# Attention scores kept negated, with a running minimum in place of a running maximum

## The chip, the cores and the metric

The kernel runs on one core of one Trainium2 chip. The metric is device time in microseconds. In the rows, PE is TensorE (PEld its weight loads), DVE is VectorE, ACT is ScalarE, POOL is GpSimd and SP is SyncE, which issues the DMAs; a "q" behind an engine's name is its sequencer.

## The reference, cut to what matters

One layer of a streaming encoder: an input projection, a short convolution beside four heads of differential attention, an output projection, a feed-forward block and a gated embedding. There are 2048 prompt rows and 32 sample rows. The part that the change touches is the softmax of the prompt's attention. Each head has two score maps (m = 0, 1):

```python
s = jnp.einsum('bqhmd,bkhmd->bhmqk', qf, kf)
dist = jnp.abs(q_pos[:, None] - k_pos[None, :]).astype(f)
bias = -alibi_slopes()[:, None, None] * dist
visible = (k_pos[None, :] // CHUNK) <= (q_pos[:, None] // CHUNK)
s = jnp.where(visible, s + bias[None, :, None], NEG_INF)
a = jax.nn.softmax(s, axis=-1)
attn = a[:, :, 0] - lam * a[:, :, 1]
o = jnp.einsum('bhqk,bkhd->bqhd', attn, v.astype(f))
```

## The kernel before, in words

**Stages.** The kernel first normalises and turns the prompt rows and projects them (to about 140 us), then does the attention of the four heads, woven with the projections of the next columns (about 140 to 895 us), and then the output projection, the feed-forward block and the gated embedding. Matrix products use pairs of 16-bit halves (high and low part), so that each product is three matmuls.

**A unit of attention.** `Unit(j, qb, idx)` is one head and one block of 128 query rows, so there are 4 x 16 units with two maps each, 128 maps in all. `scores` goes over a map's keys in chunks of at most 512 columns (320 chunks in all). Each chunk is two matmuls into a PSUM tile `sc` (three buffers; L617 and L618) and one DVE instruction, a custom `tensor_tensor_reduce` (L621). That one adds the position bias, multiplies by the head's scale `idd`, writes the scores `s` to SBUF and folds the largest of them into the [128, 1] tile `mx`, starting from the largest of the chunk before (`prev`) or from a constant in a map's first chunk. Reading the folded value out is a second DVE instruction in the trace. After the last chunk of a map POOL negates the maximum into `nm` (L628, recorded under the helper `ts`, L100), and ACT takes the exponential of the whole map with `nm` as its bias and sums it into `z` (L629).

**What follows a map.** Once both maps of a unit are there, `weigh` works out factors on POOL and DVE from the two `z` (tiles `ca`, `rz`, `sg`, `sgc`, `kk`; recorded at L102 and L583 to L586). In most units (`by_dma`) DVE combines the maps, ACT and DVE split them into halves (`s` at L170 and L105), a DMA on SP's queue turns them (`at`), and PE multiplies with the values (`smb`, L667 to L669) one unit later. The last seven units of head 3 turn the maps on PE (`turn_and_values`, tile `pta`). `subnorm` squares the result on ACT (`jko`, L518), takes a power on POOL (`rso`) and scales on DVE (`yg`).

**What runs beside it.** In the last seven units the fill is `early()`: the output projection's weights are split on ACT and DVE (`w`, L170 and L105, eight pairs of instructions of 128x1024) and the first two row tiles of that projection run.

**Order.** The program is traced by a planner (`schedule_with_timeline_sim=True`): it estimates times and sets the order of the instructions of every engine, by priority and by when they are ready in its estimate. A stretch at the start has its order written by hand on PE, ACT and DVE; the attention has not. Each engine works in order.

**Small tiles.** `t1` gives a [128, 1] tile of a pool with four buffers for each name (`sml1`, `bufs=4`), so the fifth `mx` takes the buffer of the first. Before the change `mx` is read by the next chunk's L621 or by POOL, and `nm` by ACT.

**Scales.** `q_scales` makes [128, 1] factors on POOL once for each head, among them `idd`.

Of the kernel before, what the change touches and what calls it, by code (L numbers as in the profile page):

```python
# [11 lines left out]
AF = mybir.ActivationFunctionType  # L12
ALU = mybir.AluOpType
# [16 lines left out]
BIG = 3.0e38  # L30
# [4 lines left out]
def hymba_step_kernel(  # L35
# [9 lines left out]
    V, A, G, T = nc.vector, nc.scalar, nc.gpsimd, nc.tensor  # L45
# [16 lines left out]
    cst = ctx.enter_context(tc.tile_pool(name="cst", bufs=1))  # L62
# [19 lines left out]
    def t1(tag, n=1, bufs=None):  # L82
        return here["small"].tile([P, n], F32, tag=tag, name=tag, bufs=bufs)
# [14 lines left out]
    def ts(eng, out, a, s1, op0, s2=None, op1=None):  # L98
        if op1 is None:
            eng.tensor_scalar(out=out, in0=a, scalar1=s1, scalar2=None, op0=op0)  # L100
        else:
            eng.tensor_scalar(out=out, in0=a, scalar1=s1, scalar2=s2, op0=op0, op1=op1)  # L102
# [4 lines left out]
    MUL, ADD, SUB, MAX = ALU.mult, ALU.add, ALU.subtract, ALU.max  # L107
# [55 lines left out]
    def prod(a, b, tag, c=1.0, pool=None):  # L163
        o = (pool or here["small"]).tile([P, 1], F32, tag=tag, name=tag)
        ts(G, o, a, b, MUL, c, MUL)
        return o
# [72 lines left out]
    gain = {}  # L239
# [86 lines left out]
    def k_group(c, tg, parts=1):  # L326
        j, h = c.j, heads[c.j]
        if tg == 0:
            h["ks"] = [pkv[j % 2].tile([P, S], F16, tag=f"ks{m}", name=f"ks{m}") for m in range(2)]
            h["ek"] = cst.tile([P, 1], F32, tag=f"ek{j % 2}", name="ek")  # L330
            h["swk"] = cst.tile([P, 1], F32, tag=f"swk{j % 2}", name="swk")
            G.tensor_copy(h["ek"], c.e)
            G.tensor_copy(h["swk"], c.sw)
            q_scales(order[place[GQ, j]])
# [62 lines left out]
    def q_scales(c):  # L397

        j, h = c.j, heads[c.j]
        h["iwq"] = cst.tile([P, 1], F32, tag=f"iwq{j % 2}", name="iwq")  # L400
        G.tensor_copy(h["iwq"], c.iw)
        a_ = prod(c.sw, h["swk"], "dd_a", 2.0 ** -37)
        a_ = prod(a_, gain["su"], "dd_b")
        h["dd"] = prod(a_, gain["su"], f"dd{j % 2}", 1.0, cst)
        a_ = prod(c.e, h["ek"], "id_a", 2.0 ** 9)
        a_ = prod(a_, gain["isu"], "id_b")
        h["idd"] = prod(a_, gain["isu"], f"idd{j % 2}", 1.0, cst)
        if j > 0:
            h["ratio"] = prod(h["dd"], heads[j - 1]["idd"], f"rat{j % 2}", 0.25, cst)

# [182 lines left out]
    class Unit:  # L593
# [13 lines left out]
        def scores(self):  # L607
            h, nk, qb = heads[self.j], self.nk, self.qb
            qs, q = h[("qs", qb // 4)], slice(qb % 4 * P, (qb % 4 + 1) * P)
            self.s, self.z = [], []  # L610
            for m in range(2):
                s_ = att.tile([P, S], F32, tag="s", bufs=4, name=f"s{m}")
                prev = None
                for c0, w_ in self.chunks:
                    ps = psc.tile([P, TG], F32, tag="sc", bufs=3, name="sc")
                    kc = h["ks"][m][:, c0:c0 + w_]
                    T.matmul(ps[:, :w_], qs[:, 2 * m, q], kc, start=True, stop=False)  # L617
                    T.matmul(ps[:, :w_], qs[:, 2 * m + 1, q], kc, start=False, stop=True)  # L618
                    mx = t1("mx")
                    b0 = S - nk + c0  # L620
                    ev = V.tensor_tensor_reduce(out=s_[:, c0:c0 + w_], in0=ps[:, :w_], in1=bias[:, b0:b0 + w_],  # L621
                                                scale=h["idd"], scalar=-BIG if prev is None else prev,
                                                op0=ADD, op1=MAX, accum_out=mx)
                    here["ev"] = getattr(ev, "ins", ev)
                    prev = mx
                    if c0 + w_ == nk:
                        nm, zz = t1("nm"), t1(f"z{m}")
                        ts(G, nm, prev, -1.0, MUL)  # L628
                        A.activation(out=s_[:, :nk], in_=s_[:, :nk], func=AF.Exp, bias=nm, accum_out=zz)  # L629
                        self.s.append(s_)  # L630
                        self.z.append(zz)
                    yield
# [234 lines left out]
    bias = att.tile([P, S], F32, tag="bias", bufs=1, name="bias")  # L867
# [983 lines left out]
```

## Time and profile before

| | us |
|---|---|
| median of 3 runs | 2536.61 (2534.45 to 2539.05) |
| the profiled execution, whole | 2533.34 |
| its span, first to last instruction | 2531.6 |
| PE busy in the span | 2456.3 |
| DVE busy | 1692.4 |
| ACT busy | 1139.1 |
| POOL busy | 756.0 |

The durations below come from the one profiled execution. Busy time counts overlapping instructions of an engine once. An idle time is put down to the engine and line that ended it. The granted clock is 1.00 at 2.4 GHz and 0.50 at 1.2 GHz.

### The profile page before, as it was taken

The numbers are of one execution on the slowest core, as the hardware profiler recorded it, in microseconds if no ns is written. First come the engines' busy times: TensorE is split into PE (matmuls) and PEld (weight loads), VectorE is DVE, ScalarE is ACT, GpSimd is POOL, SyncE is SP. The second block draws the span as 40 slices with busy tenths as digits, with TensorE's granted clock in tenths as the row PEclk, the third lists the DMA queues.
The fourth block names the chain that finished last, engine by engine and source line by source line (L and its number), as shares of the span: only waits on it lengthen the run. The fifth ranks groups of instructions, "written<-read, shape, count | busy, mean of one in ns | idle before, by whom it ended". The sixth has DMA issues, their size and how long they took to land.

```text
span 2531.6 us, 41709 instructions
## 1 busy us (share of the span) xinstructions
PE 2456.3 (97%) x15981; PEld 1283.6 (51%) x15981; DVE 1692.4 (67%) x2931; ACT 1139.1 (45%) x1977; POOL 756.0 (30%) x1307
## 2 busy tenths in 40 slices
PE   8999999999999799999999999999999999999998
PEld 7756655755745444444444444444444444444444
DVE  7578978969988857866665665654455547646664
ACT  5436635635643645643443443454233223425553
POOL 2143344334333434422222222210121102314442
PEclk9999999999999799999999999999999999999999
DMA  5134534524544335454444444366554547631221
GB/s 181 52 84 96 103 81 89 117 61 103 123 104 107 87 120 162 165 209 164 167 160 158 158 175 137 129 243 219 197 193 148 175 152 248 214 96 60 79 84 55
DMA packets 345083, 345.35 MB, mean 136 GB/s; under 512 B 150473, under 2 KB 241042, under 8 KB 344882
## 3 DMA queue, kind: packets, MB, share of 16 engines
q1 hardware_dynamic: 344882, 342.68, 44.4%
q8 instruction: 125, 2.05, 0.3%
q14 instruction: 76, 0.62, 0.1%
HBM read 206.68 MB, written 97.92 MB: 120 GB/s over the span
## 4 chain that ended last, share of the span: by engine, by line
PE 79%; DVE 9%; DMA 5%; ACT 3%; issue 3%; POOL 2%; SPq 0%; DVEq 0%; POOLq 0%; ACTq 0%
PE mm L1383 8%; PE mm L1385 8%; PE mm L1384 8%; PE mm L1614 7%; PE mm L1616 7%; PE mm L1615 7%; PE mm L959 4%; PE mm L961 4%; PE mm L963 4%; PE lin L317 4%; PE lin L318 4%; PE lin L319 4%; DVE s L105 2%; DVE s L621 2%; PE sc L617 1%
## 5 line engine op out<-in xcount | busy, mean ns | idle before, releaser
L1616 PE MATMUL mm<-v,hl 128*128 128x512 f16 x896 | 339.8, 380 | 3.1 <-DVE hl L1576 3.1
L1614 PE MATMUL mm<-v,hl 128*128 128x512 f16 x896 | 339.3, 380 | 2.1 <-ACT hl L1575 2.0
L1615 PE MATMUL mm<-v,hl 128*128 128x512 f16 x896 | 340.3, 380 | 0.0
L317 PE MATMUL lin<-uh,whl 128*128 128x512 f16 (+1 forms) x832 | 261.6, 330 | 4.1 <-DVE yt L105 1.3
L318 PE MATMUL lin<-ul,whl 128*128 128x512 f16 (+1 forms) x832 | 262.2, 330 | 0.7 <-DVE ul L105 0.7
L1576 DVE TENSOR_TENSOR hl<-fr,hl 128x1024 f16<-128x1024 f32 x112 | 150.0, 1349 | 168.1 <-ACT hl L1575 167.2
L319 PE MATMUL lin<-uh,whl 128*128 128x512 f16 (+1 forms) x832 | 261.7, 330 | 0.7 <-DVE whl L105 0.7
L1575 ACT ACTIVATE hl<-fr 128x1024 f16<-128x1024 f32 x112 | 116.7, 1051 | 301.7 <-PE mm L1616 278.2
L629 ACT ACTIVATE s<-s,nm 128x128 f32<-128x128 f32 (+15 forms) x128 | 153.5, 1199 | 167.1 <-POOL nm L100 166.4
L1383 PE MATMUL mm<-u,w 128*128 128x512 f16 x448 | 169.8, 379 | 1.1 <-ACT w L170 1.1
L1384 PE MATMUL mm<-u,w 128*128 128x512 f16 x448 | 169.8, 379 | 0.0
L1384 PE MATMUL mm<-u2b,w 128*128 128x512 f16 x448 | 169.8, 379 | 0.0
L1383 PE MATMUL mm<-u2b,w 128*128 128x512 f16 x448 | 169.2, 379 | 0.5 <-DMA u2b<-u_d 0.5
L1385 PE MATMUL mm<-u,w 128*128 128x512 f16 x448 | 168.8, 379 | 0.0
L1385 PE MATMUL mm<-u2b,w 128*128 128x512 f16 x448 | 168.5, 379 | 0.0
L621 DVE CUSTOM_DVE_ANT_0 s<-sc,bias,mx 128x512 f32<-128x512 f32 (+3 forms) x192 | 134.9, 702 | 16.0 <-PE sc L618 11.8
L1614 PEld LDWEIGHTS <-hl 128*128 128x128 f16 x896 | 87.8, 98 | 112.2 <-issue 6.9
L1616 PEld LDWEIGHTS <-hl 128*128 128x128 f16 x896 | 87.7, 98 | 110.7 <-DVE hl L1576 4.9
L1385 PEld LDWEIGHTS <-w 128*128 128x128 f16 x896 | 87.7, 98 | 105.3
L1615 PEld LDWEIGHTS <-hl 128*128 128x128 f16 x896 | 87.7, 98 | 104.5 <-issue 1.5
L1383 PEld LDWEIGHTS <-w 128*128 128x128 f16 x896 | 88.7, 99 | 100.2 <-ACT w L170 1.2
L1384 PEld LDWEIGHTS <-w 128*128 128x128 f16 x896 | 87.7, 98 | 99.2 <-issue 0.8
(464 smaller groups left out, 5847.8 us busy)
## 6 DMA issues: line engine op xcount, KB each, us to landing
ff_d<-e SPq DMA_DIRECT2D x224, 256.0 KB, 2.1
fr<-ff_d SPq DMA_DIRECT2D x112, 512.0 KB, 4.5
raw<-in_w_down_dram SPq DMA_DIRECT2D x80, 512.0 KB, 4.7
xt<-in_x_prompt_dram SPq DMA_DIRECT2D x32, 512.0 KB, 4.4
stg<-in_w_up_dram SPq DMA_DIRECT2D x16, 1024.0 KB, 6.5
stgd<-in_w_down_dram SPq DMA_DIRECT2D x16, 1024.0 KB, 5.6
stg<-in_w_in_dram SPq DMA_DIRECT2D x24, 512.0 KB, 5.3
h_d<-ht SPq DMA_DIRECT2D x16, 512.0 KB, 2.9
```

Source lines behind the costliest of these rows:

```text
L317: T.matmul(o, w[:, 0, ft], rh[:, ft, c], start=(ft == 0), stop=False)
L318: T.matmul(o, w[:, 0, ft], rl[:, ft, c], start=False, stop=False)
L319: T.matmul(o, w[:, 1, ft], rh[:, ft, c], start=False, stop=(ft == FT - 1))
L621: ev = V.tensor_tensor_reduce(out=s_[:, c0:c0 + w_], in0=ps[:, :w_], in1=bias[:, b0:b0 + w_], scale=h["idd"], scalar=-BIG if prev is None ...
L629: A.activation(out=s_[:, :nk], in_=s_[:, :nk], func=AF.Exp, bias=nm, accum_out=zz)
L1383: T.matmul(o, w[:, c, 0, kt], x[:, :, 0, kt], start=first and kt == 0, stop=False, skip_group_check=True)
L1384: T.matmul(o, w[:, c, 0, kt], x[:, :, 1, kt], start=False, stop=False, skip_group_check=True)
L1385: T.matmul(o, w[:, c, 1, kt], x[:, :, 0, kt], start=False, stop=kt == 3, skip_group_check=True)
L1576: V.tensor_tensor(out=hl[:, 1], in0=fr, in1=hl[:, 0], op=SUB)
L1614: T.matmul(ps, hl[:, 0, u % 2, c], v[:, 0], start=(u == 0), stop=False)
L1615: T.matmul(ps, hl[:, 0, u % 2, c], v[:, 1], start=False, stop=False)
L1616: T.matmul(ps, hl[:, 1, u % 2, c], v[:, 0], start=False, stop=(u == NU - 1))
```

## The change

The scale of the scores gets a minus sign (`nidd`), the fold becomes a minimum that starts from +3e38, and the exponential multiplies its input by -1 and adds the minimum itself: exp(-s' + min s') with s' = -s. POOL's negation and the tile `nm` go. One POOL instruction for each head is added, which makes `nidd`; `idd` stays, since the next head's `ratio` uses it.

```diff
         h["idd"] = prod(a_, gain["isu"], f"idd{j % 2}", 1.0, cst)
+        h["nidd"] = prod(a_, gain["isu"], f"nidd{j % 2}", -1.0, cst)
...
-                                                scale=h["idd"], scalar=-BIG if prev is None else prev,
-                                                op0=ADD, op1=MAX, accum_out=mx)
+                                                scale=h["nidd"], scalar=BIG if prev is None else prev,
+                                                op0=ADD, op1=ALU.min, accum_out=mx)
...
-                        nm, zz = t1("nm"), t1(f"z{m}")
-                        ts(G, nm, prev, -1.0, MUL)
-                        A.activation(out=s_[:, :nk], in_=s_[:, :nk], func=AF.Exp, bias=nm, accum_out=zz)
+
+                        zz = t1(f"z{m}")
+                        A.activation(out=s_[:, :nk], in_=s_[:, :nk], func=AF.Exp, bias=prev, scale=-1.0, accum_out=zz)
```

## Rows read from the trace of the kernel before

**Rows 1.** The page, part 1: busy us, share of the span, instructions.

```profile
PE 2456.3 (97%) x15981; PEld 1283.6 (51%) x15981; DVE 1692.4 (67%) x2931; ACT 1139.1 (45%) x1977; POOL 756.0 (30%) x1307
```

**Rows 2.** Windows: stretch, length, busy PE, PEld, DVE, ACT, POOL, clock, DMA share, GB/s.

```profile
140.00:810.00 670.00, 650.11 (x5429) 389.08 (x5427) 564.86 (x1367) 346.95 (x651) 269.12 (x605) 1.00 0.44 95
810.00:895.00 85.00, 64.19 (x433) 38.33 (x432) 63.90 (x159) 52.04 (x111) 36.97 (x96) 0.84 0.38 101
1200.00:2532.00 1332.00, 1317.12 (x6913) 604.80 (x6910) 764.94 (x988) 527.64 (x824) 313.77 (x383) 1.00 0.46 155
```

**Rows 3.** Waits of PE, 140 to 810 us: total us, times, longest.

```profile
PE smb L667 <- DMA at<-s: 6.5, 9, 1.1
PE sc L617 <- DVE mx L621: 4.2, 8, 1.0
```

**Rows 4.** Waits of PE, 810 to 895 us.

```profile
PE smb L667 <- DVE yg L100: 8.8, 3, 6.0
```

**Rows 5.** The chain that ended last: start us, us, what.

```profile
162.92 0.18 POOL nm L100
...
860.96 1.22 POOL nm L100
```

**Rows 6.** Groups by form, 140 to 895 us: busy us, mean ns, idle before.

```profile
L100 POOL TENSOR_SCALAR nm<-mx 128x1 f32<-128x1 f32 x128 | 39.1, 306 | 171.4 <-DVE mx L621 151.4 <-DVE e_w L100 10.7 <-DVE mcv L910 4.1
L621 DVE CUSTOM_DVE_ANT_0 s<-sc,bias,mx 128x512 f32<-128x512 f32 x120 | 96.3, 802 | 12.9 <-PE sc L618 10.5
L621 DVE CUSTOM_DVE_ANT_0 s<-sc,bias,idd 128x512 f32<-128x512 f32 x104 | 77.2, 743 | 5.1 <-PE sc L618 3.8 <-DMA at<-s 1.0
L364 ACT COPY kt<-ptk 128x512 f32<-128x512 f32 x12 | 6.9, 579 | 0.4 <-PE ptk L363 0.3
L170 ACT ACTIVATE at<-pta 128x512 f16<-128x512 f32 x4 | 2.4, 590 | 0.1
```

**Rows 7.** Timeline: start us, us, engine, line, out<-in, idle before.

```profile
821.92 0.08 DVE L621 DVE_READ_ACCUMULATOR2_ANT mx<- 128x1 f32 x1
822.09 0.22 POOL L100 TENSOR_SCALAR nm<-mx 128x1 f32<-128x1 f32 x1 [1.15 <-DVE mx L621]
822.35 1.25 ACT L629 ACTIVATE s<-s,nm 128x1152 f32<-128x1152 f32 x1 [3.85 <-POOL nm L100]
822.59 0.75 DVE L105 SCALAR_TENSOR_TENSOR s<-s,sgc,s 128x512 f32<-128x512 f32 x1
...
829.84 0.13 DVE L102 TENSOR_SCALAR i_wo<-e_wo 128x1 int32<-128x1 int32 x1
830.01 4.26 ACT L170 ACTIVATE w<-wst,i_wo 128x1024 f16<-128x1024 f32 x4 [0.42 <-DVE i_wo L102]
```

**Rows 8.** Timeline at 861 us, DVE and POOL.

```profile
860.82 1.28 DVE L105 SCALAR_TENSOR_TENSOR w<-wst,aswo,w 128x1024 f16<-128x1024 f32 x1
860.93 1.24 POOL L100 TENSOR_SCALAR nm<-mx 128x1 f32<-128x1 f32 x1
```

**Rows 9.** Waits of DVE, 140 to 810 us.

```profile
DVE rz L583 <- ACT s L629: 17.3, 18, 2.2
```

**Rows 10.** The tile idd on POOL: ns min/median/max, first and last start.

```profile
L102 POOL TENSOR_SCALAR idd<-id_b,g_i x4: 263/266/1322, 80.3 to 597.2; 128x1 f32<-128x1 f32 x4
```

**Rows 11.** Timeline: an exponential, and the fourth eviction after its maximum.

```profile
730.37 1.90 ACT L629 ACTIVATE s<-s,nm 128x1920 f32<-128x1920 f32 x1 [0.24 <-POOL nm L100]
...
733.13 0.52 DVE L621 CUSTOM_DVE_ANT_0 s<-sc,bias,mx 128x256 f32<-128x256 f32 x1
```

**Rows 12.** Timeline at 835 us, ACT and PE.

```profile
835.31 4.25 ACT L170 ACTIVATE w<-wst,aswo 128x1024 f16<-128x1024 f32 x4
839.47 0.26 ACT L518 ACTIVATE jko<-smb 128x128 f16<-128x128 f32 x1
...
841.53 0.27 PE L667 MATMUL smb<-vhl,at 128*128 128x128 f16 x1 [6.04 <-DVE yg L100]
```

**Rows 13.** Windows: the longest stretch of half clock there, columns of Rows 2.

```profile
836.22:846.46 10.24, 4.90 (x34) 3.71 (x34) 5.56 (x13) 7.85 (x16) 3.55 (x8) 0.50 0.30 58
```

## The prediction, as it was put on record

> **What bounds the kernel now.** I read the page's shares first: PE is busy for 97% of the span [rows 1], so an edit on DVE, POOL and ACT can win at most what PE lacks, and only where those engines make PE wait. The windows say where that is [rows 2]. From 1200 us on PE is busy for 1317.12 of 1332 us, and nothing of the change runs there. The attention falls into two parts. From 140 to 810 us PE is idle for 670 - 650.11 = 19.9 us at full clock, while DVE is busy for 564.86 of 670 us (84%). From 810 to 895 us, which I call the tail, PE is idle for 85 - 64.19 = 20.8 us, and the granted clock is 0.84 on the mean. So some 41 us of idle time, and what the half clock costs in the tail, are all that the change can reach.
>
> The waits of PE tell who holds it up. Before 810 us it waits 6.5 us in all for the turned maps `at`, which come out of the exponentials by way of combining, splitting and a DMA, and 4.2 us for a free `sc` buffer, which DVE's evictions give back [rows 3]. In the tail the largest is 8.8 us for `yg` [rows 4]. None of these names `nm`: POOL's negation is at least two steps away from PE. The chain of waits shows how often it matters all the same. I went through it from 140 to 900 us and found POOL's `nm` in 15 pieces, 5.64 us together; the first and the last stand in [rows 5]. The other 113 of the 128 are not on it.
>
> **The change part by part.**
>
> *The negation goes.* There are 128 of them, 39.1 us of POOL [rows 6]; POOL has idle time enough, so that alone is worth nothing. What counts is when the exponential starts. In the timeline the read-out of the maximum ends at 822.00, `nm` runs from 822.09 to 822.31 and the exponential starts at 822.35 [rows 7]: 0.35 us from DVE to ACT. Where ACT waits for DVE directly, DVE's `i_wo` ends at 829.97 and ACT starts at 830.01 [rows 7], which is 0.04 us. So a map whose exponential waits for `nm` gains 0.31 us. A further gain is the hold: `nm` at 860.93 takes 1.24 us instead of 0.22, and it ends 0.07 us after a DVE instruction that began 0.11 us before it and reads two tensors of SBUF [rows 8]. That is why the mean is 306 ns [rows 6] and the pieces on the chain are 5.64 us and not 15 x 0.22 = 3.3 us.
>
> The Trainium skill's page "SBUF — State Buffer" (section "Who interferes with whom") states the reason: a DVE instruction with two SBUF inputs contends with a GpSimd instruction that reads SBUF. By a price without it the chain's pieces would be 3.3 us, and with it they are the 5.64 us that the trace has; the trace agrees with the page.
>
> At the order as it is, the most that can go is the chain's pieces plus the longer way to POOL: 5.64 + 15 x (0.09 + 0.04 - 0.04) = 7.0 us. The least is nothing, where another path was as late. What is late next can be named. In the part before 810 us it is DVE: it stands 17.3 us, 18 times, at the head of `weigh` (`rz`) waiting for an exponential [rows 9], and 18 x 0.31 = 5.6 us of this goes; but the combining and splitting behind it is DVE's own work, 84% of the stretch. At 860.96 it is DVE's split of the weights, which runs anyway [rows 8]. With DVE so close behind, I take half of the upper end: -3.5 us.
>
> *The fold becomes a minimum.* 320 DVE instructions change their operation; the trace has no such form. Both sides are bounded by the two forms that it has, 743 ns with a constant as start and 802 ns with a tile, for 512 columns [rows 6]: 59 x 320 = 18.9 us of DVE time more or less. I take nothing, because another two-input instruction with a multiplication and an addition also takes 0.75 us for 512 columns [rows 7]: the columns set the time and not the operation. The read-out stays, 0.08 us [rows 7].
>
> *The exponential gets a scale of -1.* Its nearest rows are a copy without a factor, 579 ns, and a copy with a constant factor, 590 ns, on 512 columns [rows 6]: 11 x 128 = 1.4 us of ACT as the upper end, nothing as the lower. ACT is busy for 347 of 670 us [rows 2], which hides it; without that cover it would be the 1.4 us. I take 0.
>
> *`nidd` is added.* Four POOL instructions of 0.27 us like `idd` [rows 10], 1.1 us in all, or 5.3 us if each met the longest hold (1.32). They are made while the keys of a head are projected, ahead of the head's first unit; POOL is busy for 40% there. I take 0.
>
> *`mx` is held longer.* It is now freed by the exponential's end, and there are four buffers. So an L621 waits for the exponential of the map whose last chunk lies four chunks back. I set each of these 124 pairs side by side: the closest is an exponential that ends at 732.27 and an eviction at 733.13 [rows 11], so no pair would wait at today's times, by 0.86 us. If one waited, all of DVE's queue behind it (combining, splits, further evictions) and PE's `sc` would wait with it. I take 0, with up to 1 us for each pair that slips by 2 us.
>
> *The order may move.* The planner sets the order of PE, ACT and DVE by its own estimate, in which the exponentials are now ready earlier. No row shows the new order. A price for one misplaced block is in the tail: four splits of the weights, 4.25 us, stand on ACT before the square `jko`, and PE is idle for 6.04 us until `yg` [rows 12]; over the next 10.24 us the clock is at half while PE is busy for 4.90 us, work that takes half of that at full clock, so it costs 2.45 us [rows 13]. One such block is 4.25 + 2.45 = 6.7 us, in either direction. I take 0, since nothing in the rows says which way it goes.
>
> **Sum.** -3.5 + 0 + 0 + 0 + 0 + 0 = -3.5 us on the profiled execution, 2533.34 us (span 2531.6 and 1.74 us around it), so 2529.8 us there. The median of the runs shown is 3.3 us above that execution, so the prediction for a median is 2536.6 - 3.5 = 2533.1 us. About what a measurement of this kernel can tell from no change is 0.2%, or 5.1 us, so this is a gain inside it.
>
> **The rivals.**
>
> *The gain is all covered.* The 15 pieces go, and DVE is as late as before. For it: DVE is busy for 84% [rows 2], and the waits of PE name evictions and transfers [rows 3]. Against it: 18 waits of DVE end with an exponential [rows 9]. The time stays at 2536.6 us.
>
> *A better order in the tail (faster).* Exponentials that are ready sooner let the planner put `jko` ahead of the block of four splits. For it: the tail has 20.8 us of idle PE, by far the largest share of any stretch. Against it: the splits don't depend on `nm`. It is worth -6.7 us, and -10.2 where the chain's pieces, which were counted in the order as it is, can be had on top: 2526.4 to 2529.9, so some 2528 us.
>
> *A worse order in the tail (slower).* Exponentials that are ready sooner go before other ACT work, and the other four splits, too, land before a square that PE waits for. That is one block more, +6.7 us, and in another order the chain's pieces don't carry over: 2543.3 us. It decides from 5.1 us on, three quarters of a block with its clock. For it: the rows show that one such block costs PE 6 us. Against it: there are only eight splits, and four already stand badly.
>
> *The buffers of `mx` bind (slower).* If exponentials slip by 2 us against evictions, the closest pair waits 1.1 us; some eight such pairs give +9 - 3.5 = +5.5 us: 2542 us. Against it: exponentials come earlier by the change, not later.
>
> *The minimum runs at another speed (slower).* At 59 ns more, 18.9 us of DVE time, of which PE would see perhaps half, an estimate from DVE's 84%: +9.5 - 3.5 = +6 us, 2542.6 us.
>
> **How the numbers follow.** The forecast gets 0.37, the covered gain 0.11, the better order 0.30, the worse order 0.15, the buffers 0.04 and the slower minimum 0.03. Of the forecast's 0.37 the part beyond -5.1 us (its upper end is -7.0) is 0.03. So faster by over 0.2%: 0.30 + 0.03 = 0.33; within 0.2%: 0.34 + 0.11 = 0.45; slower: 0.15 + 0.04 + 0.03 = 0.22. The likeliest is the forecast, 2533.1 us; its own range is 2529.6 to 2536.6 us. The range takes in the better order below, to 2524 us (its far end and another 2.4 us, one more stretch of half clock saved), and the three slower rivals above, to 2545 us.
>
> **What would show it right or wrong.** No `nm` on POOL and 0.04 us from the read-out to the exponential; L621 still at 743 and 802 ns; `rz` waiting some 5 us less; PE's idle time before 810 us down by two or three us; no L621 that waits for an exponential. The order of ACT in the tail says whether one of the two order rivals came about: how long `yg` keeps PE waiting, and how long the clock is at half. The prediction is wrong if PE's idle time between 140 and 895 us moves by more than about 8 us either way, and then the order of an engine's instructions will have moved and not the price of one.

## The result, and the profile after

The changed kernel is slower: a median of 2551.81 us (2550.49 to 2558.08, 4 runs) against 2535.55 us (2534.45 to 2539.05, 4 runs) for the kernel before on the same chip, a ratio of 1.0066 with a 95% interval of 1.0054 to 1.0078. The forecast was 2533.1 us, and the time lies 7 us above the upper end of its range.

In the rows of after, all lines behind L407 have one number more than in those of before. First part 1 of the page:

```profile
PE 2462.5 (97%) x15981; PEld 1287.3 (51%) x15981; DVE 1693.2 (66%) x2931; ACT 1139.0 (45%) x1977; POOL 716.1 (28%) x1183
```

POOL has 124 instructions less (128 negations gone, four `nidd` added) and 39.9 us less to do. DVE and ACT have what they had [rows 1]. PE does the same 15981 instructions in 6.2 us more. The groups by form, from 140 to 905 us, have the prices of the changed parts:

```profile
L622 DVE CUSTOM_DVE_ANT_0 s<-sc,bias,mx 128x512 f32<-128x512 f32 x120 | 96.3, 803 | 11.0 <-PE sc L619 8.5 <-DVE mx L622 0.2
L622 DVE CUSTOM_DVE_ANT_0 s<-sc,bias,nidd 128x512 f32<-128x512 f32 x104 | 77.1, 743 | 10.6 <-PE sc L619 7.0 <-PE pta L696 1.7 <-DMA at<-s 1.5
...
L102 POOL TENSOR_SCALAR nidd<-id_b,g_i 128x1 f32<-128x1 f32 x3 | 1.5, 487 | 0.0
```

The minimum costs what the maximum did, 803 and 743 ns for 802 and 743 [rows 6], and none of the idle time ahead of an L622 was ended by an exponential. ACT's busy time did not move. So the changed instructions cost what was forecast, but for `nidd` with a mean of 0.49 us instead of 0.27 (three of its four stand here). The windows and the waits did not come out so. The same three stretches as in [rows 2]:

```profile
140.00:810.00 670.00, 644.72 (x5360) 385.88 (x5359) 557.49 (x1350) 343.01 (x644) 231.98 (x493) 0.99 0.44 94
810.00:895.00 85.00, 64.50 (x445) 38.95 (x444) 67.64 (x163) 49.52 (x100) 32.46 (x70) 0.86 0.41 105
1200.00:2532.00 1332.00, 1323.99 (x6945) 608.10 (x6944) 766.65 (x988) 528.88 (x824) 312.19 (x383) 1.00 0.46 156
```

PE's waits from 140 to 810 us, where [rows 3] had 4.2 us for `sc` and 6.5 us for `at`:

```profile
PE sc L618 <- DVE mx L622: 14.3, 11, 3.1
PE smb L668 <- DMA at<-s: 4.1, 4, 1.8
```

DVE's waits at the head of `weigh`, over the whole attention (140 to 920 us; before has 17.3 us, 18 times, in this window as in [rows 9]):

```profile
DVE rz L584 <- ACT s L630: 11.0, 14, 1.9
```

The way that the change shortens did get shorter. At 725 us the read-out of the minimum ends at 724.98 + 0.07 = 725.05 and the exponential starts 0.06 us later, where it took 0.35 us by way of POOL [rows 7]:

```profile
724.98 0.07 DVE L622 DVE_READ_ACCUMULATOR2_ANT mx<- 128x1 f32 x1
```

```profile
725.11 1.88 ACT L630 ACTIVATE s<-s,mx 128x1920 f32<-128x1920 f32 x1
```

DVE waits 6.3 us less for exponentials, close to the 5.6 us of the part-by-part working, and `at` is waited for 2.4 us less. But before 810 us PE's idle time went from 19.9 to 25.3 us, and the wait for a free `sc`, which DVE's evictions give back, more than trebled.

The longest of these waits shows what that looks like. DVE's timeline (start us, us, engine, line, instruction), and then PE's:

```profile
724.98 0.73 DVE L622 CUSTOM_DVE_ANT_0 s<-sc,bias,nidd 128x512 f32<-128x512 f32 x1
725.65 0.07 DVE L622 DVE_READ_ACCUMULATOR2_ANT mx<- 128x1 f32 x1
725.65 0.73 DVE L105 SCALAR_TENSOR_TENSOR s<-s,sg,s 128x512 f16<-128x512 f32 x1
726.31 1.20 DVE L906 TENSOR_REDUCE wmax<-wst 128x1 f32<-128x1024 f32 x1
727.44 1.39 DVE L105 SCALAR_TENSOR_TENSOR s<-s,sg,s 128x512 f16<-128x512 f32 x2
728.76 1.20 DVE L906 TENSOR_REDUCE wmax<-wst 128x1 f32<-128x1024 f32 x1
729.89 0.73 DVE L105 SCALAR_TENSOR_TENSOR s<-s,sg,s 128x512 f16<-128x512 f32 x1
730.55 0.79 DVE L622 CUSTOM_DVE_ANT_0 s<-sc,bias,mx 128x512 f32<-128x512 f32 x1
```

```profile
727.94 0.33 PE L619 MATMUL sc<-ks,qs 128*128 128x384 f16 x1
731.40 0.38 PE L618 MATMUL sc<-ks,qs 128*128 128x512 f16 x1 [3.14 <-DVE mx L622]
...
736.28 0.38 PE L618 MATMUL sc<-ks,qs 128*128 128x512 f16 x1 [0.77 <-DVE mx L622]
736.50 0.38 PE L619 MATMUL sc<-ks,qs 128*128 128x512 f16 x1
739.57 0.58 PE L618 MATMUL sc<-ks,qs 128*128 128x512 f16 x1 [2.69 <-DVE mx L622]
```

DVE is busy without a break, but its queue has 4.9 us of splits and `wmax` between two evictions, and PE stands for 3.14 us with its three `sc` buffers full. A second such wait follows at 736.88, and from 737.10 the clock is at half: the matmul of 0.38 us takes 0.58, and the windows view gives for that stretch

```profile
737.10:743.90 6.80, 4.33 (x30) 3.24 (x30) 6.80 (x17) 5.22 (x9) 2.44 (x6) 0.50 0.20 38
```

No instruction here belongs to the change. What is new is the order. Against the kernel before, 3598 of PE's 15853 ordered instructions stand at another place (by up to 306 places), 758 of DVE's 2603 (by up to 48), 256 of ACT's 1634 (by up to 11), 101 of SP's 970 and 236 of POOL's 1175; none of those on PE, DVE and ACT behind the output projection. The planner was given an exponential that is ready sooner and queued everything anew. The experiments are about that.

### The profile page after: what moved, and what is told of

Its sections match the earlier page's. It is cut to its first block, busy times and chain, and to the rows that moved or that the text cites. A ratio compares the mean times of both kernels' runs of the same rounds, so it can differ in the third digit from the quotient of the medians.

```text
span 2548.7 us, 41565 instructions
## 1 busy us (share of the span) xinstructions
PE 2462.5 (97%) x15981; PEld 1287.3 (51%) x15981; DVE 1693.2 (66%) x2931; ACT 1139.0 (45%) x1977; POOL 716.1 (28%) x1183
## 4 chain that ended last, share of the span: by engine, by line
PE 77%; DVE 9%; DMA 5%; issue 3%; ACT 3%; POOL 2%; SPq 0%; DVEq 0%; POOLq 0%; ACTq 0%
PE mm L1384 8%; PE mm L1386 8%; PE mm L1385 8%; PE mm L1615 6%; PE mm L1617 6%; PE mm L1616 6%; PE mm L960 5%; PE mm L962 5%; PE mm L964 5%; PE lin L317 4%; PE lin L319 3%; PE lin L318 3%; DVE s L105 2%; DVE s L622 2%; PE sc L618 1%
## 5 line engine op out<-in xcount | busy, mean ns | idle before, releaser
L630 ACT ACTIVATE s<-s,mx 128x128 f32<-128x128 f32 (+15 forms) x128 | 153.5, 1199 | 166.4 <-DVE mx L622 164.7
L622 DVE CUSTOM_DVE_ANT_0 s<-sc,bias,mx 128x512 f32<-128x512 f32 (+3 forms) x192 | 135.1, 703 | 16.6 <-PE sc L619 11.7
```

## The experiments

In several of them the order is pinned: each instruction gets a dependency, without a semaphore, on the one of its engine that is to stand ahead of it, which sets the order of the queue. The order is taken from another kernel's program, instruction by instruction. POOL's `nm` and `nidd`, which only one of the kernels has, are left to the planner. A kernel pinned to its own order was not run, so what pinning alone costs was not measured; e1, the fastest kernel here, leaves it little room.

```diff
         hymba_step_kernel(tc, *args)
+        pin_order(tc, nc)
```

### Edit and order apart

**e1_new_in_old_order**: the changed kernel, pinned to the order of before.

> The changed kernel, with the instructions of every engine queued in the order that they had before the change (the negation gone, the new scale added). Theory A (the order that the planner made is what costs 16 us): no slower than before, 2530 to 2536 us, with the gain of at most 7 us that the chain of waits allowed. Rival B (the shorter way itself, the minimum or the scale of -1 costs): as slow as the changed kernel, some 2550 us.

Measured: 2530.77 us (2528.53 to 2533.32) beside 2536.76, ratio 0.9979 (0.9970 to 0.9988). It is the fastest kernel of this study, faster than both that were given, and within theory A's range. In its trace every engine runs the instructions that both kernels have in the order of before.

**e2_old_in_new_order**: the kernel before, pinned to the order of the changed one.

> The kernel before, with the instructions of every engine queued in the order that they have after the change; only the negations are placed by the planner. Theory A (the order): as slow as the changed kernel or a little slower, 2550 to 2557 us. Rival B (the edit itself): as before, 2536 us.

Measured: 2571.39 us (2565.40 to 2574.43), ratio 1.0139 (1.0123 to 1.0154). Rival B falls; theory A had the sign, but its range ended 14 us too low.

So the edit gains in either order (6.0 us in the old one, 19.6 in the new one), and the new order loses with either set of instructions. With no negation it costs 2551.81 - 2530.77 = 21.0 us, with one 2571.39 - 2536.76 = 34.6 us. By stages, after first and then e1, which runs the same instructions; the bounds are the first eviction of each head, the first matmul of the up-projection and the end (stretch, length, busy PE, PEld, DVE, ACT, POOL, clock, DMA share, GB/s):

```profile
147.16:308.76 161.60, 154.79 (x1381) 96.38 (x1378) 142.80 (x359) 93.91 (x182) 59.69 (x135) 1.00 0.48 98
308.76:492.59 183.83, 178.61 (x1554) 109.78 (x1551) 154.93 (x380) 97.01 (x187) 70.16 (x149) 1.00 0.44 91
492.59:699.82 207.23, 201.24 (x1694) 121.16 (x1692) 165.61 (x403) 103.79 (x198) 70.53 (x152) 0.98 0.44 97
699.82:904.49 204.67, 173.43 (x1181) 97.44 (x1180) 163.42 (x381) 99.83 (x187) 68.97 (x141) 0.92 0.40 95
904.49:1079.90 175.41, 170.52 (x885) 84.41 (x884) 125.79 (x163) 91.31 (x191) 68.12 (x115) 0.97 0.46 150
1079.90:2548.70 1468.80, 1450.90 (x7674) 667.41 (x7671) 850.95 (x1111) 586.60 (x922) 344.95 (x418) 1.00 0.46 157
```

```profile
147.25:305.61 158.36, 155.05 (x1368) 96.00 (x1364) 143.25 (x361) 93.65 (x181) 57.90 (x133) 1.00 0.48 101
305.61:485.65 180.04, 176.47 (x1548) 108.85 (x1546) 153.30 (x379) 97.38 (x190) 71.62 (x150) 1.00 0.44 92
485.65:688.10 202.45, 196.26 (x1685) 119.58 (x1683) 165.03 (x399) 103.05 (x197) 66.97 (x151) 1.00 0.45 98
688.10:884.76 196.66, 174.18 (x1208) 96.93 (x1206) 161.59 (x380) 99.12 (x186) 68.68 (x138) 0.93 0.41 98
884.76:1057.74 172.98, 168.88 (x892) 83.95 (x890) 127.18 (x166) 92.03 (x194) 69.48 (x119) 0.99 0.47 155
1057.74:2526.66 1468.92, 1450.13 (x7674) 666.83 (x7671) 850.81 (x1111) 586.36 (x922) 345.01 (x418) 1.00 0.46 157
```

Everything from the up-projection on takes the same 1468.8 us. The loss is in all five stages before: 3.2 + 3.8 + 4.8 + 8.0 + 2.4 = 22.2 us. PE's idle time in them is 54.15 us in after and 39.65 in e1 (length less busy), which is 14.5 us more; the other 7.8 us are PE's busy time, more for the same work. Most of those are the clock: in these stages after has 47.8 us at half clock with PE busy for 35.7 us of them, e1 30.7 us with 21.9, and half of the difference is 6.9 us, an estimate from these windows. At the place of the 3.14 us above, DVE's queue in e1 is

```profile
716.25 2.72 DVE L105 SCALAR_TENSOR_TENSOR s<-s,sg,s 128x512 f16<-128x512 f32 x4
718.90 1.20 DVE L906 TENSOR_REDUCE wmax<-wst 128x1 f32<-128x1024 f32 x1
720.03 0.79 DVE L622 CUSTOM_DVE_ANT_0 s<-sc,bias,mx 128x512 f32<-128x512 f32 x1
720.76 0.07 DVE L622 DVE_READ_ACCUMULATOR2_ANT mx<- 128x1 f32 x1
720.76 1.20 DVE L906 TENSOR_REDUCE wmax<-wst 128x1 f32<-128x1024 f32 x1
```

with the eviction between the two `wmax`, and PE waits 1.00 us.

### Parts of the edit

**e3_sign_alone**: the sign, the minimum and the scale, with POOL's instruction kept as a copy.

```diff
-h["idd"] = prod(a_, gain["isu"], f"idd{j % 2}", 1.0, cst)
+h["idd"] = prod(a_, gain["isu"], f"idd{j % 2}", -1.0, cst)
...
-    ts(G, nm, prev, -1.0, MUL)
-    A.activation(out=s_[:, :nk], in_=s_[:, :nk], func=AF.Exp, bias=nm, accum_out=zz)
+    ts(G, nm, prev, 1.0, MUL)
+    A.activation(out=s_[:, :nk], in_=s_[:, :nk], func=AF.Exp, bias=nm, scale=-1.0, accum_out=zz)
```

> The sign and the minimum alone: negated scale, running minimum, exponential with a scale of -1, and the POOL instruction kept as a copy of the minimum that the exponential reads, so that the way from DVE over POOL to ACT and the order stay as before. Theory A: within 0.2% of before, 2533 to 2539 us. Rival C (the minimum or the scale runs slower): over 5 us slower.

Measured: 2534.62 us, ratio 0.9996 (0.9986 to 1.0006). The planner gives exactly the order of before. The minimum and the scale cost nothing that these runs can tell: the interval goes from 3.6 us less to 1.5 us more.

**e4_pool_kept_unread**: as e3, but the exponential reads `prev` itself, so that POOL's copy is made and read by nobody.

```diff
-    A.activation(out=s_[:, :nk], in_=s_[:, :nk], func=AF.Exp, bias=nm, scale=-1.0, accum_out=zz)
+    A.activation(out=s_[:, :nk], in_=s_[:, :nk], func=AF.Exp, bias=prev, scale=-1.0, accum_out=zz)
```

> The changed kernel, with a POOL instruction of the old kind after each map whose result nobody reads, and with the sign in idd itself and not in a second tile. The exponential reads the minimum directly, and the planner makes a third order. Theory A: a third time, anywhere from 2530 to 2560 us, that goes with the idle time of PE in the attention; a rival by which POOL's freed time is the cause would have it back at 2536 us.

Measured: 2545.47 us (2541.75 to 2546.58), ratio 1.0035 (1.0023 to 1.0048). POOL is as busy as before and the kernel is still slower than before, so the loss does not need POOL's freed time; e1, where POOL has it, is faster. The planner made a third order here.

### Which engine, which head

**e5_dve_order** and **e6_pe_order**: `pin_order` holds one engine to the order of before, DVE or PE; the planner places the rest.

> The changed kernel with DVE alone queued in the order that it had before; the planner places the other engines around it. Theory A (what costs is DVE's order: longer runs of combining and splitting between two evictions, so that PE waits for a free sc): most of the 21 us of the new order comes back, 2530 to 2537 us, and PE's waits for sc between 140 and 920 us fall from 21 us to about 12. Theory B (what costs is PE's own order, the scores and projections put elsewhere): PE still has a new order here, so the time stays near 2545 to 2552 us. Theory C (ACT's order costs, the exponentials and squares): also 2545 us or more.

> The changed kernel with PE alone queued in the order that it had before; the planner places the other engines around it. Theory A (DVE's order costs): the planner has to follow PE's demand for evictions, so DVE's order moves by at most a dozen places, but it still moves; some of the 21 us stays, 2535 to 2545 us. Theory B (PE's own order costs): 2530 to 2534 us. Theory C (ACT's order): 2545 us or more, as ACT's order differs from before in 190 places.

Measured: 2560.07 us (ratio 1.0087, 1.0073 to 1.0100) and 2562.69 us (1.0108, 1.0095 to 1.0121). Holding DVE or PE alone gave nothing back, so theories A and B missed: e6 is slower than the changed kernel, and e5 too by the medians, though the intervals overlap. With DVE in its old order PE's waits for `sc` did fall, from 21.3 to 14.1 us, and other waits took their place (`yg` 13.9 us for 9.4). But in both runs the planner drew the other engines' orders anew: in e5 154 of ACT's and some 2000 of PE's instructions stand elsewhere than before, in e6 190 of ACT's and 551 of DVE's. So these are a fourth and a fifth order, and no single engine is shown to carry the loss or to be free of it. Theory C (ACT's order), whose 2545 us or more fits both times, stays open.

**e7_new_order_heads_0_to_2** and **e8_new_order_from_head_3**: all engines change from one order to the other at the start of the last head.

> The changed kernel; every engine has the new order up to the start of the last head and the order of before from there on. Theory D (the new order costs a little in every head): the loss of heads 0 to 2 stays, 3.2 + 3.8 + 4.7 = 11.7 us by the stages of the two profiles, so about 2542 us. Theory E (a worse order in the tail alone, as the prediction's rival had it): 2531 us, as with the whole order of before.

> The reverse: the order of before up to the start of the last head, the new order from there on. Theory D: the loss of the last head and of the output projection stays, 8.0 + 2.4 = 10.4 us, so about 2541 us. Theory E: the whole loss of 21 us, 2552 us.

Measured: 2548.69 us (1.0051, 1.0038 to 1.0064) and 2537.79 us (1.0008, 0.9999 to 1.0017). Above e1 that is 17.9 and 7.0 us, together some 4 us more than the 21. Theory E falls: the tail alone is not it, and the larger part is in heads 0 to 2. Theory D holds in kind, but its sizes, from the stages of one profile each, were 7 us too low for e7 and 3 us too high for e8. Stages of one profile are no more exact than about 4 us: heads 0 to 2 take 556.6 us in the profile of e7 and 552.7 us in that of after, in the same order.

### Are late evictions the cause?

**e9_evictions_forward** and **e10_forward_in_old_order**: single evictions moved forward in DVE's queue, at each place where PE had waited for `sc`. At 725 us, for one:

```diff
  read-out of mx                (725.65)
+ eviction 128x512              (was at 730.55)
  split s, wmax, split s x2, wmax, split s
- eviction 128x512
```

> The changed kernel in its own new order on every engine, but in DVE's queue 20 of the 320 evictions stand 1 to 7 instructions further forward. They are those at the 18 places where PE waited for a free sc between 140 and 920 us (21.3 us in all in the changed kernel's profile); each goes ahead of the combining and splitting that stood between it and the end of its matmul. Nothing else differs. Theory A (evictions stuck behind combining work are what costs): PE's waits for sc fall below 10 us, some of the half clock behind them goes too, and the time falls by 10 us or more, to 2530 to 2542 us. Theory H (DVE has no time to spare: what is put back then delays the turned maps or yg by as much): the waits change their name and the time stays at 2547 to 2553 us.

> The changed kernel in the order of before (2530.8 us), with 14 evictions put forward in the same way, at the places where PE waited for sc in that run (12.1 us in 14 pieces between 140 and 920 us). Theory A: 2520 to 2527 us. Theory H: 2529 to 2533 us.

Measured: 2557.17 us (1.0085, 1.0072 to 1.0099) and 2540.51 us (1.0008, 0.9998 to 1.0019), 5 and 10 us slower than without the moves by the medians (the interval of e9 overlaps that of the changed kernel, that of e10 lies clear of e1's). PE's waits in e9, 140 to 920 us:

```profile
PE smb L668 <- DVE yg L100: 13.5, 3, 7.9
PE pty L578 <- DVE sbig L100: 6.5, 2, 3.9
PE pos L573 <- DVE sbig L566: 4.4, 1, 4.4
...
PE sc L618 <- DVE mx L622: 3.5, 8, 1.0
```

The waits for `sc` went from 21.3 to 3.5 us, just as intended, but `yg` went from 9.4 to 13.5 us, and `sbig` came up with 6.5 + 4.4 = 10.9. Theory A falls. Theory H is right that the waits change their name, but both times lie above its ranges (2553 and 2533 us at most), so the moves cost more than they gave. Here the line that PE waits longest for was a symptom: taking most of that wait away did not make the kernel faster.

### An exponential that is late against its plan

**e11_negation_twice** is the kernel before with a second negation, which makes the exponential later in the planner's estimate; **e12_negation_twice_old_order** pins it to the order of before.

```diff
     ts(G, nm, prev, -1.0, MUL)
+    ts(G, nm, prev, -1.0, MUL)
```

> The kernel before, with POOL's negation written twice in a row for each map (the same value into the same tile); the planner sets the order again, with exponentials that are later in its estimate and not earlier. It moves 3484 of PE's and 753 of DVE's instructions against before. Theory F (the order of before is a good one, and any new order costs, whichever way the exponentials move): 2545 us or more. Theory G (only earlier exponentials make a bad order): the second negation alone, nothing to 128 x 0.22 / 4 = 7 us, so 2536 to 2543 us.

> The same with every engine's order as it was before, so the second negation's own price: 15 pieces on the chain by 0.22 us, 3.3 us, and up to 7 us where more maps come onto it: 2536 to 2543 us. What the run before has above this one is its order's (theory F: 5 us or more; theory G: nothing).

Measured: 2552.78 us (1.0065, 1.0052 to 1.0079) and 2556.46 us (1.0079, 1.0066 to 1.0092). The time of e11 lies in theory F's range, but not for its reason: the same instructions in the old order are no faster. Theory G is right that the new order costs nothing here, but both times lie far above its 2543 us, because I had given the second negation 7 us at most; in the unchanged order it costs 19.9 (2556.46 less the 2536.6 of before). In e12 DVE waits more at `rz`:

```profile
DVE rz L583 <- ACT s L630: 27.2, 29, 2.5
```

That is 29 waits, where before had 18 [rows 9], so DVE stands waiting for maps that it did not wait for with one negation. How these waits add up to 19.9 us is not shown: the chain of e12 can be followed back only to 685 us. And the planner's new order for two negations is not worse than the old one: 3.7 us faster by the medians, with intervals that overlap.

So two theories were left, and three more runs completed a table of three instruction sets by three orders: **e13_no_negation_in_order_for_two**, **e14_one_negation_in_order_for_two** and **e15_two_negations_in_order_for_none**, all by `pin_order`.

> The changed kernel (no negation), every engine in the order that the planner made for two negations. Theory F (the order of before is an unusually good one, any other costs): 2540 to 2560 us, as the other orders of these instructions. Theory L (an order that was made for a later exponential leaves room, one made for an earlier one leaves none): below the 2536.6 us of before. By the steps of the old order (2556.5 with two negations, 2536.6 with one, 2530.8 with none) taken from the 2552.8 us that this order gives with two: 2552.8 - 19.9 - 5.8 = 2527 us.

> The kernel before (one negation) in the order made for two. Theory F: above 2540 us. Theory L: 2552.8 - 19.9 = 2533 us, up to 2538 us.

> Two negations in the order made for none. Theory L: the worst of all, some 20 us above the 2571.4 us that one negation takes in this order, 2585 to 2600 us. Theory F says nothing of the negations, only that this order costs some 15 to 35 us more than that of before with the same instructions (2556.5 us): 2571 to 2592 us.

Measured: 2536.20 us (0.9993, 0.9984 to 1.0002), 2538.37 us (1.0004, 0.9996 to 1.0013) and 2597.49 us (1.0229, 1.0209 to 1.0248). The table of medians in us, with DVE's wait at `rz` for an exponential (140 to 920 us) behind it:

| order made for | no negation | one | two |
|---|---|---|---|
| none | 2551.8, 11.0 | 2571.4, 22.2 | 2597.5, 36.4 |
| one | 2530.8, 8.9 | 2536.6, 17.3 | 2556.5, 27.2 |
| two | 2536.2, 5.6 | 2538.4, 11.3 | 2552.8, 19.4 |

The middle of the table is the median shown ahead of the prediction; beside the runs of this study the kernel before stood at 2534.7 to 2537.6 us. Its two corners, as the views of the waits have them:

```profile
DVE rz L583 <- ACT s L630: 36.4, 34, 2.5
```

```profile
DVE rz L584 <- ACT s L630: 5.6, 7, 1.6
```

(e15, and e13.) Theory F falls: the order of before is not the only good one, since the one made for two negations comes within 0.2% of the kernel before with no negation and with one. Theory L is borne out for the order made for none: that is the slowest for each set of instructions, by 16 to 45 us, and a negation costs most in it, 19.6 us from none to one (5.8 and 2.2 in the other two orders) and 26.1 from one to two (19.9 and 14.4). Between the orders made for one and for two the intervals overlap with each set of instructions, so that part of the sequence is not shown. Its sizes were right for e15, missed by 0.4 us for e14, and were too hopeful for e13 (2527 us forecast, 2536.2 measured, not clearly below before), because it took the steps of one order over to another.

**e16_new_order_rz_back** and **e17_old_order_rz_forward**: is the room at one place enough? In DVE's queue, in 26 units:

```diff
  last eviction of the unit's second map
- rz = 1 / z
  other work (evictions, splits)
+ rz = 1 / z
```

and the reverse in e17.

> The changed kernel in its own new order, with one kind of instruction moved: 26 of the 57 `rz` (the first of DVE's instructions that needs the exponential of a unit) stand 1 to 5 instructions further back, so that DVE has more other work between a map's last eviction and `rz` (a mean of 2.08 us by the durations of the instructions, for 1.73 in this order and 2.19 in that of before). Theory L, with the room at `rz` as what counts: DVE's waits at rz fall from 11.0 us to 8 or less, and half of the 21 us or more comes back, 2531 to 2541 us. Theory M (the room at `rz` is only one sign of a plan that is too tight at many places): 2546 us or more.

> The reverse: the changed kernel in the order of before (2530.8 us), with the same 26 `rz` 1 to 8 instructions further forward, so that the room falls from 2.19 to 1.51 us, less than the new order's 1.73. Theory L with the room at `rz`: DVE's waits at rz rise from 8.9 us to 15 or more and the time goes up by 10 us or more, to 2541 us or above. Theory M: 2530 to 2537 us.

Measured: 2565.35 us (1.0112, 1.0092 to 1.0131) and 2540.03 us (1.0014, 1.0005 to 1.0023). Against the same order without the moves, taking the room away costs 9 us, and giving it costs 14 us. In e16 DVE's waits (140 to 920 us) are

```profile
DVE s L105 <- POOL sgc L102: 12.3, 33, 0.6
DVE rz L587 <- POOL ca L102: 8.2, 18, 1.5
DVE rz L584 <- ACT s L630: 7.8, 9, 1.9
```

where after has 3.9 us for `sgc` and 4.4 for `ca`. `rz` waits less, 7.8 for 11.0 us, and the steps behind it, which go by POOL and back, wait more. In e17 the wait rose as theory L had it, from 8.9 us to

```profile
DVE rz L584 <- ACT s L630: 24.5, 25, 2.2
```

and the time came 1 us short of its forecast and 3 us above theory M's. So the room at `rz` counts in the old order. But it is not what the new order loses: e17 waits there for 24.5 us and is 12 us faster than the changed kernel, which waits for 11.0. By that and by e16, theory L in the form that the room at `rz` decides falls. Theory M fits e16 and missed e17; that the new order is tight along the whole way from the maximum to the split is a reading of e16's rows, and not shown.

## Why the prediction was wrong

**The negation goes, -3.5 us.** Right in kind. In an order that is the same on both sides the medians are 6.0 us apart, and the interval of the ratio gives 3 to 8 us. The upper end, 7.0 us from the chain's pieces, was nearer than the half that I took; both lie in the interval. It is not a bound in general: the same sum on e2 (34 pieces of `nm` on the chain, 10.9 us) gives 14.0 us, and there the negation's going is worth 19.6 by the medians. The next-late path that I named (DVE at `rz`) did give way: 17.3 to 8.9 us in e1, where I expected some 5 less.

**Minimum, scale, `nidd`, `mx`: nothing.** Right, by e3 (0.9996), by the rows of L622 (803 and 743 ns) and by an L622 that never waits for an exponential. `nidd` takes 487 ns in after and not 270, but there are only four. The 1.4 us for the scale's upper end counted each map as 512 columns; by the maps' columns it would be 272 x 11 ns = 3.0 us, and ACT's busy time shows neither.

**"The order may move ... I take 0, since nothing in the rows says which way it goes."** This is the step that failed. I gave a term nothing because its sign was not known, and it was worth +21 us, six times the largest term of the sum (-3.5 us). The rival for it ("a worse order in the tail") had the sign, but its place and price were wrong: the wait for `yg`, its mark, went only from 8.8 to 9.4 us, and it looked at one block of four weight splits on ACT in the tail and gave it 6.7 us. e8 shows 7.0 us for the last head and what follows, and e7 shows 17.9 us for heads 0 to 2, where the prediction gave the order no price at all. With the 0.15 that I gave it and its 2543.3 us, the range ended 7 us too low. The sign that I had set for being wrong would not have caught it either: PE's idle time between 140 and 895 us went from 40.7 to 45.8 us, less than the 8 us that I asked, since at 895 us the changed kernel still has some of its attention ahead.

Some rows could have warned me. DVE is busy 84% of the stretch [rows 2] and waits 18 times for an exponential [rows 9]: these waits can be read as a queue that already runs a little ahead of the real exponentials, so that one drawn for still earlier ones could run further ahead; that is argued and not shown. I read them only as time to be won. The table shows besides that a path whose negation is worth 6 us when it goes costs 19.9 us when it is doubled: a price for shortening the path did not carry over to lengthening it.

**What stays open.** Why the planner's order for no negation is the worse one was not settled. That it is worse with all three sets of instructions is shown; that it is tight at many places between the maximum and the split is only suggested by e16 (`sgc` and `ca`). Whether the planner's estimate of the exponential is too early by a fixed amount, so that any earlier one must overshoot, is only argued. Which engine's order carries the loss, ACT's among them (theory C), is open too: mixing the two orders, an engine at a time with nothing planned anew, wasn't tried.

## What to carry to other kernels

When a planner sets the order, an edit that shortens one path is two changes: the path and the order. Price them apart by holding the order (here -6 and +21 us), and keep the old order with the new instructions if that is the faster pair. When predicting, give a redrawn order a price of its own over the whole stage, not over the one place where a wait is long today: the orders that the planner made anew, in whole or in part, for the kernels whose exponential reads the minimum itself (after, e4, e5, e6) came out 9 to 28 us slower than before, though the edit alone gains 6. Waits of a busy engine at the head of a dependent run may be a sign that its queue is planned too close.

## What the runs showed of the hardware that I had not expected

An instruction of 0.29 us on POOL with a single element per partition (the mean of the 256 `nm` in e12), added once for each of 128 maps, cost 19.9 us of the whole kernel with the order held, though POOL had been busy for only 30% of the span [rows 1]. And PE's longer waits were paid for twice: against e1, after has 14.5 us more of idle time and 7.8 us more of busy time for the same work, of which some 6.9 us go with its 17 us more at half clock. The granted clock fell to half behind such waits, as at 737.10 us, after 3.14 us and in a wait of 2.69 us.
